# Holding back the PSUM eviction of the first MLP product, and splitting the first weight tiles in halves

## The chip, the core and the metric

The kernel runs on one core of a Trainium2 chip. The metric is the device time of one execution in microseconds (us), lower is better. Matrix products run on TensorE, which has a queue for weight loads beside the one for matmuls (PEld and PE in the profile). ScalarE (ACT) and VectorE (DVE) do the elementwise work, SyncE (SP) issues nearly all loads, and every engine works through its own instructions in a fixed order. TensorE writes into PSUM banks, from which ScalarE and VectorE take the results.

## What is computed

The reference is a decoder trunk of two layers for 256 tokens and a width of 2048. Only the MLP part and the frame around it matter here:

```
def _sqrelu_mlp(h, w1, w2):
    return jnp.square(jax.nn.relu(h @ w1)) @ w2

def reference(x, ...):
    for l in range(DEPTH):            # DEPTH = 2
        h = _rmsnorm(x, norm1_g[l])
        ...                           # layer 0: convolution and differential attention
        ...                           # layer 1: forgetting attention
        h = _rmsnorm(x, norm2_g[l])
        x = x + _sqrelu_mlp(h, mlp_w1[l], mlp_w2[l])   # hidden width 8192
    return x
```

## The kernel before

All products are made with float32 accuracy out of a fast format: each operand is split into a high part and a low part, and three matmuls (high by high, high by low, low by high) are added up in PSUM. For a weight tile `raw` of 1 MB, `split_w` writes the high part `wh` on ScalarE (line 136) and the low part `wl` on VectorE (line 137). There are three buffers each for `raw`, `wh` and `wl`, so a split waits until TensorE has finished with the tile three places earlier, and a load waits until the tile three places earlier is split.

The MLP (`mlp`) goes over the hidden width in four groups `g` of 2048. In each group `hidden` makes the first product in eight pairs of 128-column blocks: `gemm_t` loads and splits two weight tiles per pair, runs their matmuls (lines 548 and 552) and leaves two PSUM banks `acc[0]` and `acc[1]`. Taking them out is called eviction here. It is a copy on ScalarE (line 597) and an add on VectorE (line 598) for each bank, then ReLU and square in one VectorE instruction (line 600), then `p.fill`, which splits the result for the second product (for the last pair lines 582 and 583):

```
fj = f[:, 2 * j:2 * j + 2].rearrange("p t n -> p (t n)")
nc.scalar.copy(fj, acc[j][:, 2 * P:])
nc.vector.tensor_tensor(fj, acc[j][:, :2 * P], fj, ALU.add)
```

The second product (`gemm_pair`) follows, twice per group, for `n` = 0 and `n` = 2. It goes over the same eight pairs, one weight tile each. Pairs of kind S use a product scheme with seven products instead of eight. It needs sums of weight blocks, a tile `T` that VectorE builds in three instructions (lines 632, 634, 635) and that is split like a weight tile. So an S tile has two splits, `wa` of the loaded tile and `wb` of `T`. On TensorE an S tile is 21 matmuls (lines 615 to 617), of which the first nine use `wa` and the other twelve `wb`; a C tile is 24. The tiles come in the order S C S C S C C C, 183 matmuls in all. Four banks, `P2`, `Q3`, `Q4` and `X`, come from the same pool of four as the `acc` banks of the first product: `Q4` and `X` are the two that the last pair of `hidden` has just filled.

`late` is a list of work that is postponed; `flush()` does it. `gemm`, `gemm_t` and `gemm_pair` call `flush()` behind the split of their first weight tile and ahead of their first matmul. A scheduler then orders the instructions of each engine; it keeps to the data but may move an instruction past others. So the order of the program is not simply the order of the code.

At the start of the kernel the first product loads its first weight tile in two halves (`first=True`, line 150) but splits it in one piece.

Of the kernel before, what the change touches and what calls it, by code (L numbers as in the profile page):

```python
# [8 lines left out]
F32 = mybir.dt.float32  # L9
F32R = mybir.dt.float32r  # L10
AF = mybir.ActivationFunctionType
ALU = mybir.AluOpType
# [4 lines left out]
P = 128  # L17
D = 2048
KT = D // P
CW = 512  # L20
# [6 lines left out]
def trunk_kernel(  # L27
# [7 lines left out]
    nc = tc.nc  # L35
# [6 lines left out]
    qkv = ctx.enter_context(tc.tile_pool(name="qkv", bufs=2))  # L42
# [34 lines left out]
    late = []  # L77

    def flush():

        while late:
            late.pop(0)()

    def step():

        while pending:
            try:
                next(pending[0])
                return True
            except StopIteration:  # L90
                pending.pop(0)
        return False

    def until(done):
        while not done():
            assert step()
# [31 lines left out]
                nc.vector.scalar_tensor_tensor(lo, src, scalar, hi.bitcast(F32), ALU.mult, ALU.subtract)  # L128
            self.left -= n

    def split_w(src, shape=(4, CW)):

        n = src.shape[1]
        wh = wspl.tile([P, *shape], F32R, name="wh")[:, :n]
        wl = wspl.tile([P, *shape], F32R, name="wl")[:, :n]
        nc.scalar.copy(wh, src)  # L136
        nc.vector.tensor_tensor(wl, src, wh.bitcast(F32), ALU.subtract)  # L137
        return wh, wl

    def gemm(acts, w, c0, first=False):  # L140

        acc = []
        total = 4 * len(acts)
        i = 0
        for ai, a in enumerate(acts):
            raw = wraw.tile([P, 4, CW], F32, name="raw")
            src = w[a.row:a.row + CW, c0:c0 + CW].rearrange("(k p) n -> p k n", p=P)
            if first and ai == 0:
                for h in range(2):
                    nc.sync.dma_start(raw[:, 2 * h:2 * h + 2, :], src[:, 2 * h:2 * h + 2, :])  # L150
            else:
                nc.sync.dma_start(raw, src)
            wh, wl = split_w(raw)
            if i == 0:
                flush()
                acc += [accp.tile([P, CW], F32, name="acc") for _ in range(2)]
            until(lambda: a.left <= 0)
            for h in range(2):
                for t in range(2):
                    ts = slice(t * P, (t + 1) * P)  # L160
                    for k in (2 * h, 2 * h + 1):
                        st, sp = i + k == 0, i + k == total - 1
                        nc.tensor.matmul(acc[t], a.hi[:, k, ts], wh[:, k, :], start=st, stop=False)  # L163
                        nc.tensor.matmul(acc[t], a.hi[:, k, ts], wl[:, k, :], start=False, stop=False)  # L164
                        nc.tensor.matmul(acc[t], a.lo[:, k, ts], wh[:, k, :], start=False, stop=sp)  # L165
                step()
            i += 4
        return acc
# [38 lines left out]
    def proj(nm, w, c0, name, first=False):  # L207

        acc = gemm(nm.acts, w, c0, first)
        if name == "q":  # L210
            qk_tile.append(qkv.tile([P, 4, CW], F32, name="qk"))
        o = qkv.tile([P, 2, CW], F32, name="v") if name == "v" else \
            qk_tile[-1][:, (0 if name == "q" else 2):(2 if name == "q" else 4), :]
        for t in range(2):
            nc.scalar.activation(o[:, t, :], acc[t], AF.Copy, scale=nm.r(t))
        return o
# [302 lines left out]
    def out_proj(acts, w, nxt):  # L519

        for part in (acts[:-1], acts[-1:]):
            for n in range(NCH):
                acc = gemm(part, w, n * CW)
                for t in range(2):
                    nc.vector.tensor_tensor(xr[n][:, t, :], acc[t], xr[n][:, t, :], ALU.add)
                if len(part) == 1:
                    pending.append(nxt.chunk(n))

    def gemm_t(acts, w, c0):


        acc = []
        for c in range(2):
            raw = wraw.tile([P, 8, 2 * P], F32, name="raw")
            r0 = c * 8 * P
            nc.sync.dma_start(raw, w[r0:r0 + 8 * P, c0:c0 + 2 * P].rearrange("(k p) n -> p k n", p=P))
            wh, wl = split_w(raw, (8, 2 * P))
            if c == 0:
                flush()
                acc += [accp.tile([P, CW], F32, name="acc") for _ in range(2)]  # L540
            for h in range(2):
                a = acts[2 * c + h]
                until(lambda: a.left <= 0)
                for f in range(2):
                    fs = slice(f * P, (f + 1) * P)
                    for k in range(4):
                        st = c + h + k == 0
                        nc.tensor.matmul(  # L548
                            acc[f], wh[:, 4 * h + k, fs], a.both[:, k, :, :].rearrange("p s t -> p (s t)"), start=st, stop=False)
                    for k in range(4):  # L550
                        sp = (c, h, k) == (1, 1, 3)
                        nc.tensor.matmul(acc[f][:, 2 * P:], wl[:, 4 * h + k, fs], a.hi[:, k, :], start=False, stop=sp)  # L552
                step()
        return acc
# [34 lines left out]
    def hidden(nm, w, c0):  # L589

        pairs, half = [], None
        for i, kind in enumerate(KINDS):
            acc = gemm_t(nm.acts, w, c0 + 2 * i * P)
            f = qkv.tile([P, 4, CW], F32, name="qk")[:, :2].rearrange("p a (f n) -> p (a f) n", n=P)
            for j in range(2):
                fj = f[:, 2 * j:2 * j + 2].rearrange("p t n -> p (t n)")
                nc.scalar.copy(fj, acc[j][:, 2 * P:])  # L597
                nc.vector.tensor_tensor(fj, acc[j][:, :2 * P], fj, ALU.add)  # L598
            f4 = f[:, :4].rearrange("p t n -> p (t n)")
            nc.vector.scalar_tensor_tensor(f4, f4, 0.0, f4, ALU.max, ALU.mult)  # L600
            if kind == "S":
                p = PairS()
            elif half is not None:
                p, half = PairC(half), None
            elif "C" in KINDS[i + 1:]:
                t = actp.tile([P, 4, 2, 2 * P], F32R, name="act")
                p, half = PairC(t[:, :2]), t[:, 2:]
            else:
                p = PairC(qkv.tile([P, 2, 2, 2 * P], F32R, name="v"))
            p.fill(f)  # L610
            pairs.append(p)
        return pairs

    def products(acc, a, b, started, last):
# [4 lines left out]
    def gemm_pair(pairs, w, r0, n, r2, done):  # L619
# [3 lines left out]
        for i, (kind, p) in enumerate(zip(KINDS, pairs)):  # L623
# [6 lines left out]
            if kind == "S":  # L630
                T = qkv.tile([P, 4, CW], F32, name="qk")
                nc.vector.tensor_tensor(
                    T[:, 0:2], raw[:, 1:3], raw[:, 0:1].broadcast_to([P, 2, CW]), ALU.add)
                nc.vector.tensor_tensor(T[:, 2], T[:, 1], raw[:, 1], ALU.add)
                nc.vector.tensor_tensor(T[:, 3], T[:, 2], raw[:, 3], ALU.add)  # L635
                wa, wb = split_w(raw[:, 1:4]), split_w(T)
            else:
                wa = split_w(raw)
# [41 lines left out]
    def mlp(nm, l, nxt):  # L680
        ov = out[0].rearrange("(t p) d -> p t d", p=P)
        r2 = None
        for g in range(4):
            pairs = hidden(nm, mlp_w1[l], g * D)
            if g == 0:
                r2 = small.tile([P, 2], F32, name="r2", bufs=3)
                for t in range(2):
                    nc.vector.tensor_tensor(r2[:, t:t + 1], nm.r(t), nm.r(t), ALU.mult)
            for n in (0, 2):
                def done(stage, m=None, t=None, n=n, g=g):  # L690
                    if g != 3:
                        return
                    if nxt is None:
                        if stage == 1:
                            q = nc.sync if t == 0 else nc.scalar
                            q.dma_start(ov[:, t, m * CW:(m + 1) * CW], xr[m][:, t, :])
                    elif n == 2 and stage == 0:
                        pending.extend([nxt.chunk(0), nxt.chunk(1)])
                    elif n == 2 and (m, t) == (n + 1, 1):
                        pending.extend([nxt.chunk(2), nxt.chunk(3)])  # L700
                gemm_pair(pairs, mlp_w2[l], g * D, n, r2, done)
        if nxt is None:
            flush()
# [72 lines left out]
```

## Time and profile before

| | before |
|---|---|
| device time, median of 3 runs | 2217.84 us (2216.75 to 2218.78) |
| device time of the profiled execution | 2219.12 us |
| its span, from the first to the last instruction | 2217.4 us |
| TensorE matmul busy | 2183.2 us (98%) |
| VectorE busy | 1544.1 us (70%) |
| ScalarE busy | 1051.0 us (47%) |

The profiled execution took 1.3 us longer than the median, and 1.7 us of it lie outside the span. A busy share of 98% says that TensorE has work almost always; it doesn't say that this work runs at full speed, since matmuls overlap and their recorded ends are modelled. Starts are better: in a dense stretch one matmul of 512 columns starts every 0.23 us at full clock. PEclk is the clock that TensorE was granted, as a share of 2.4 GHz.

### The profile page before, as it was taken

The page shows a single profiled execution, that of the slowest core. Times are in us where ns is not written, and L with a number is a line of the kernel's source. Part 1 is how long each engine was busy: PE and PEld are TensorE (multiplying, and loading weights), DVE is VectorE, ACT ScalarE, POOL GpSimd, SP SyncE. Part 2 cuts the span into 40 slices and gives each one's busy share as a digit, 9 for nine tenths or more (in the row PEclk, how much of TensorE's full clock was granted, in tenths as well). Part 3 has the DMA queues.
Part 4 walks back from the last instruction along what each step waited for, and adds up shares of the span by engine and source line. Part 5 has one row for each costly group of instructions (what it writes and reads, how often), then busy time and mean ns, then how long its engine had stood idle before and what let it go on. Part 6 is the DMA issues. An engine that isn't in the chain of part 4 may idle for free.

```text
span 2217.4 us, 25974 instructions
## 1 busy us (share of the span) xinstructions
PE 2183.2 (98%) x10724; PEld 1824.2 (82%) x10724; DVE 1544.1 (70%) x1568; ACT 1051.0 (47%) x1095; POOL 18.4 (1%) x17
## 2 busy tenths in 40 slices
PE   8999999999999999999999999999999999999999
PEld 6887888888887887887888888888888888878877
DVE  5576655768768768767855565657687687687677
ACT  5455444545435444444554455445454454444443
POOL 0000000000000000000000000000000000000000
PEclk9999999999999999999999999999999999999999
DMA  7544556546655665664646555556556556656654
GB/s 253 176 166 161 181 188 192 177 154 207 210 163 199 214 186 177 211 190 161 214 159 203 185 175 177 183 162 186 157 204 211 161 198 211 188 171 210 189 166 157
DMA packets 245240, 412.07 MB, mean 186 GB/s; under 512 B 9367, under 2 KB 144770, under 8 KB 245122
## 3 DMA queue, kind: packets, MB, share of 16 engines
q1 hardware_dynamic: 237264, 405.84, 56.9%
q10 hardware_dynamic: 7858, 4.58, 0.7%
q8 instruction: 84, 1.38, 0.2%
q14 instruction: 34, 0.28, 0.0%
HBM read 408.28 MB, written 2.11 MB: 185 GB/s over the span
## 4 chain that ended last, share of the span: by engine, by line
PE 96%; DVE 1%; ACT 1%; DMA 1%; issue 0%; ACTq 0%; DVEq 0%
PE acc L548 21%; PE acc L552 11%; PE acc L163 11%; PE acc L165 10%; PE acc L164 10%; PE acc L616 8%; PE acc L617 8%; PE acc L615 8%; PE tp L616 2%; PE tp L617 2%; PE tp L615 2%; ACT wh L136 1%; DVE wl L137 1%; PE tp L184 1%; PE tp L305 0%; PE tp L317 0%
## 5 line engine op out<-in xcount | busy, mean ns | idle before, releaser
L137 DVE TENSOR_TENSOR wl<-raw,wh 128x2048 fp32r<-128x2048 f32 (+1 forms) x384 | 853.5, 2223 | 453.1 <-ACT wh L136 452.7
L136 ACT CAST wh<-raw 128x2048 fp32r<-128x2048 f32 (+1 forms) x384 | 711.0, 1856 | 488.7 <-PE acc L165 218.7
L548 PE MATMUL acc<-act,wh 128*128 128x512 f32 x2048 | 559.5, 395 | 0.0
L163 PE MATMUL acc<-wh,act 128*128 128x512 f32 x1024 | 413.0, 404 | 0.3 <-ACT act L127 0.2
L164 PE MATMUL acc<-wl,act 128*128 128x512 f32 x1024 | 400.8, 391 | 0.0
L165 PE MATMUL acc<-wh,act 128*128 128x512 f32 x1024 | 400.7, 392 | 0.0
L548 PEld LDWEIGHTS acc<-act,wh 128*128 128x128 f32 x2048 | 350.3, 189 | 47.9 <-DVE act L128 0.6
L552 PEld LDWEIGHTS acc<-act,wl 128*128 128x128 f32 x2048 | 314.2, 189 | 43.4
L552 PE MATMUL acc<-act,wl 128*128 128x256 f32 x2048 | 325.7, 281 | 0.0
L616 PE MATMUL acc<-wl,act 128*128 128x512 f32 x656 | 257.2, 392 | 0.0
L617 PE MATMUL acc<-wh,act 128*128 128x512 f32 x656 | 255.8, 390 | 0.0
L615 PE MATMUL acc<-wh,act 128*128 128x512 f32 x656 | 245.8, 392 | 1.1 <-ACT wh L136 1.1
L165 PEld LDWEIGHTS acc<-wh,act 128*128 128x128 f32 x1024 | 192.5, 188 | 42.2 <-DVE act L128 0.4
L163 PEld LDWEIGHTS acc<-wh,act 128*128 128x128 f32 x1024 | 192.8, 188 | 39.2 <-issue 2.0
L164 PEld LDWEIGHTS acc<-wl,act 128*128 128x128 f32 x1024 | 193.2, 189 | 37.5 <-issue 0.7
L136 ACT CAST wh<-qk 128x2048 fp32r<-128x2048 f32 x48 | 91.7, 1910 | 211.3 <-DVE qk L635 211.3
L137 DVE TENSOR_TENSOR wl<-qk,wh 128x2048 fp32r<-128x2048 f32 x48 | 109.9, 2290 | 60.2 <-ACT wh L136 60.2
L615 PEld LDWEIGHTS acc<-wh,act 128*128 128x128 f32 x656 | 123.5, 189 | 28.8 <-ACT wh L136 2.8
L616 PEld LDWEIGHTS acc<-wl,act 128*128 128x128 f32 x656 | 123.8, 189 | 28.3 <-DVE wl L137 2.3
L617 PEld LDWEIGHTS acc<-wh,act 128*128 128x128 f32 x656 | 123.8, 189 | 25.7
L597 ACT COPY qk<-acc 128x256 f32<-128x256 f32 x128 | 47.0, 367 | 178.6 <-PE acc L552 178.6
L598 DVE TENSOR_TENSOR qk<-acc,qk 128x256 f32<-128x256 f32 x128 | 53.8, 420 | 54.7 <-ACT qk L597 54.7
(173 smaller groups left out, 1604.1 us busy)
## 6 DMA issues: line engine op xcount, KB each, us to landing
raw<-in_mlp_w_dram SPq DMA_DIRECT2D x256, 1024.0 KB, 5.4
raw<-in_fox_w_in_dram SPq DMA_DIRECT2D x48, 1024.0 KB, 5.1
raw<-in_hyb_w_in_dram SPq DMA_DIRECT2D x47, 1024.0 KB, 5.1
raw<-in_hyb_w_out_dram SPq DMA_DIRECT2D x16, 1024.0 KB, 5.1
raw<-in_fox_w_out_dram SPq DMA_DIRECT2D x16, 1024.0 KB, 5.1
ob<-fcd ACTq DMA_DIRECT2D x4, 512.0 KB, 4.6
xr<-in_x_dram SPq DMA_DIRECT2D x3, 512.0 KB, 8.1
raw<-in_hyb_w_in_dram SPq DMA_DIRECT2D x2, 512.0 KB, 6.8
```

What stands on the lines that cost most here:

```text
L136: nc.scalar.copy(wh, src)
L137: nc.vector.tensor_tensor(wl, src, wh.bitcast(F32), ALU.subtract)
L163: nc.tensor.matmul(acc[t], a.hi[:, k, ts], wh[:, k, :], start=st, stop=False)
L164: nc.tensor.matmul(acc[t], a.hi[:, k, ts], wl[:, k, :], start=False, stop=False)
L165: nc.tensor.matmul(acc[t], a.lo[:, k, ts], wh[:, k, :], start=False, stop=sp)
L548: nc.tensor.matmul(acc[f], wh[:, 4 * h + k, fs], a.both[:, k, :, :].rearrange("p s t -> p (s t)"), start=st, stop=False)
L552: nc.tensor.matmul(acc[f][:, 2 * P:], wl[:, 4 * h + k, fs], a.hi[:, k, :], start=False, stop=sp)
L597: nc.scalar.copy(fj, acc[j][:, 2 * P:])
L598: nc.vector.tensor_tensor(fj, acc[j][:, :2 * P], fj, ALU.add)
L615: nc.tensor.matmul(acc, a[0], b[0], start=not started, stop=False)
L616: nc.tensor.matmul(acc, a[0], b[1], start=False, stop=False)
L617: nc.tensor.matmul(acc, a[1], b[0], start=False, stop=last)
```

## The change

In `hidden`, the eviction of a pair becomes a function `take`, which is put on `late`. It is thus done by the next `flush()`: for pairs 0 to 6 behind the split of the next pair's first weight tile, and for pair 7 in `gemm_pair`, behind the splits of `wa` and `wb` of the second product's first tile. In `split_w`, a tile can be split in parts, and the four tiles of the kernel's first product (`first=True`) are split in two halves each.

```
-    def split_w(src, shape=(4, CW)):
+    def split_w(src, shape=(4, CW), parts=1):
...
-        nc.scalar.copy(wh, src)
-        nc.vector.tensor_tensor(wl, src, wh.bitcast(F32), ALU.subtract)
+        for i in range(parts):
+            s = slice(i * n // parts, (i + 1) * n // parts)
+            nc.scalar.copy(wh[:, s], src[:, s])
+            nc.vector.tensor_tensor(wl[:, s], src[:, s], wh[:, s].bitcast(F32), ALU.subtract)
         return wh, wl
...
-            wh, wl = split_w(raw)
+            wh, wl = split_w(raw, parts=2 if first else 1)
...
             acc = gemm_t(nm.acts, w, c0 + 2 * i * P)
-            f = qkv.tile([P, 4, CW], F32, name="qk")[:, :2].rearrange("p a (f n) -> p (a f) n", n=P)
-            for j in range(2):
...
-            p.fill(f)
             pairs.append(p)
+
+            def take(acc=acc, p=p):
+                f = qkv.tile([P, 4, CW], F32, name="qk")[:, :2].rearrange("p a (f n) -> p (a f) n", n=P)
+                for j in range(2):
+                    fj = f[:, 2 * j:2 * j + 2].rearrange("p t n -> p (t n)")
+                    nc.scalar.copy(fj, acc[j][:, 2 * P:])
+                    nc.vector.tensor_tensor(fj, acc[j][:, :2 * P], fj, ALU.add)
+                f4 = f[:, :4].rearrange("p t n -> p (t n)")
+                nc.vector.scalar_tensor_tensor(f4, f4, 0.0, f4, ALU.max, ALU.mult)
+                p.fill(f)
+            late.append(take)
         return pairs
```

Lines behind the two edits move by 2 and by 5 in the changed kernel: 136 and 137 become 138 and 139; the eviction's 597, 598 and 600 become 611, 612 and 614; 583 becomes 585; 632, 634 and 635 become 637, 639 and 640.

The first place is VectorE's order at the border between the two products, in the first group of the first MLP; it is the same in all eight groups. `qk` is the name of the buffers both of the evicted result `f` and of `T`. Before, from the split of the second product's first loaded tile on (1536 columns):

```order
L137 TENSOR_TENSOR wl<-raw,wh 128x1536
L598 TENSOR_TENSOR qk<-acc,qk 128x256
L600 SCALAR_TENSOR_TENSOR qk<-qk 128x512
L583 TENSOR_TENSOR act<-qk,act 128x2x256
L632 TENSOR_TENSOR qk<-raw 128x1024
L598 TENSOR_TENSOR qk<-acc,qk 128x256
L634 TENSOR_TENSOR qk<-qk,raw 128x512
L598 TENSOR_TENSOR qk<-acc,qk 128x256
L635 TENSOR_TENSOR qk<-qk,raw 128x512
L600 SCALAR_TENSOR_TENSOR qk<-qk 128x512
L137 TENSOR_TENSOR wl<-qk,wh 128x2048
L583 TENSOR_TENSOR v<-qk,v 128x2x256
```

In the changed kernel, from the sums of `T` of the first tile on:

```order
L637 TENSOR_TENSOR qk<-raw 128x1024
L612 TENSOR_TENSOR qk<-acc,qk 128x256
L639 TENSOR_TENSOR qk<-qk,raw 128x512
L640 TENSOR_TENSOR qk<-qk,raw 128x512
L612 TENSOR_TENSOR qk<-acc,qk 128x256
L139 TENSOR_TENSOR wl<-raw,wh 128x1536
L614 SCALAR_TENSOR_TENSOR qk<-qk 128x512
L585 TENSOR_TENSOR act<-qk,act 128x2x256
L139 TENSOR_TENSOR wl<-qk,wh 128x2048
```

The two adds among these rows (612) are now those of pair 6, whose banks were full one pair earlier. The adds of pair 7 follow only behind the split of `T` (`wl<-qk`), in this order:

```order
L637 TENSOR_TENSOR qk<-raw 128x1024
L612 TENSOR_TENSOR qk<-acc,qk 128x256
L639 TENSOR_TENSOR qk<-qk,raw 128x512
L640 TENSOR_TENSOR qk<-qk,raw 128x512
L139 TENSOR_TENSOR wl<-raw,wh 128x2048
L612 TENSOR_TENSOR qk<-acc,qk 128x256
L139 TENSOR_TENSOR wl<-raw,wh 128x1536
L614 SCALAR_TENSOR_TENSOR qk<-qk 128x512
L139 TENSOR_TENSOR wl<-qk,wh 128x2048
L585 TENSOR_TENSOR v<-qk,v 128x2x256
```

So what moved is pair 7's eviction, from between the sums of the first `T` to behind its split; it now stands among the sums of the third tile's `T` and the splits of the second and third tile. For pairs 0 to 6 the scheduler already had this order.

The second place is VectorE at the kernel's start. `g_95` and `ob` are gains and small constants, line 128 (unchanged) splits activations. Before:

```order
L128 SCALAR_TENSOR_TENSOR act<-tp,g_95,act 128x256 x4
L137 TENSOR_TENSOR wl<-raw,wh 128x2048
L128 SCALAR_TENSOR_TENSOR act<-tp,g_95,act 128x256 x4
L137 TENSOR_TENSOR wl<-raw,wh 128x2048 x2
L128 SCALAR_TENSOR_TENSOR act<-tp,g_95,act 128x256 x2
```

In the changed kernel:

```order
L128 SCALAR_TENSOR_TENSOR act<-tp,g_95,act 128x256 x3
L139 TENSOR_TENSOR wl<-raw,wh 128x1024
L128 SCALAR_TENSOR_TENSOR act<-tp,g_95,act 128x256
L139 TENSOR_TENSOR wl<-raw,wh 128x1024
L128 SCALAR_TENSOR_TENSOR act<-tp,g_95,act 128x256 x2
L139 TENSOR_TENSOR wl<-raw,wh 128x1024 x2
```

Each split of the first product is now two instructions of half the width, with activation splits between them.

## Rows read from the trace of the kernel before

**Rows 1.** The page, busy time, share of the span and instructions of TensorE.
```profile
PE 2183.2 (98%) x10724; PEld 1824.2 (82%) x10724; DVE 1544.1 (70%) x1568; ACT 1051.0 (47%) x1095; POOL 18.4 (1%) x17
```

**Rows 2.** Waits of TensorE: waiting line, releaser, us in total, times, longest.
```profile
PE tp L615 <- ACT wh L136: 10.9, 8, 1.4
PE tp L616 <- DVE wl L137: 9.1, 8, 1.1
```

**Rows 3.** Windows over second products and one pair before: stretch, us, busy (instructions), PEclk, DMA share, GB/s.
```profile
487.30:532.62 45.32, 42.52 (x185) 1.00 0.59 199
...
2124.36:2171.80 47.44, 44.94 (x185) 0.93 0.56 190
sum 367.03, PE 345.91; mean PE 43.24
...
532.62:574.33 41.71, 41.71 (x184) 1.00 0.65 212
...
476.07:487.30 11.23, 11.23 (x67) 1.00 0.24 86
```

**Rows 4.** Timeline, TensorE: start, us, instruction, idle before and releaser.
```profile
487.30 0.40 PE L615 MATMUL tp<-wh,act 128*128 128x512 f32 x1
...
490.91 0.96 PE L615 MATMUL tp<-wh,act 128*128 128x512 f32 x3 [1.39 <-ACT wh L136]
...
493.24 0.50 PE L616 MATMUL tp<-wl,act 128*128 128x512 f32 x1 [1.14 <-DVE wl L137]
```

**Rows 5.** Timeline, VectorE, around the same border.
```profile
472.40 2.29 DVE L137 TENSOR_TENSOR wl<-raw,wh 128x2048 fp32r<-128x2048 f32 x1 [1.12 <-ACT wh L136]
...
477.31 1.76 DVE L137 TENSOR_TENSOR wl<-raw,wh 128x1536 fp32r<-128x1536 f32 x1 [1.56 <-ACT wh L136]
...
481.54 1.23 DVE L632 TENSOR_TENSOR qk<-raw 128x1024 f32<-128x1024 f32 x1
486.55 0.42 DVE L598 TENSOR_TENSOR qk<-acc,qk 128x256 f32<-128x256 f32 x1 [3.78 <-ACT qk L597]
486.89 0.68 DVE L634 TENSOR_TENSOR qk<-qk,raw 128x512 f32<-128x512 f32 x1
487.90 0.42 DVE L598 TENSOR_TENSOR qk<-acc,qk 128x256 f32<-128x256 f32 x1 [0.33 <-ACT qk L597]
488.25 0.68 DVE L635 TENSOR_TENSOR qk<-qk,raw 128x512 f32<-128x512 f32 x1
...
490.89 2.29 DVE L137 TENSOR_TENSOR wl<-qk,wh 128x2048 fp32r<-128x2048 f32 x1 [1.36 <-ACT wh L136]
```

**Rows 6.** Timeline, ScalarE, around the same border.
```profile
487.50 0.37 ACT L597 COPY qk<-acc 128x256 f32<-128x256 f32 x1 [0.98 <-PE acc L552]
488.96 1.90 ACT L136 CAST wh<-qk 128x2048 fp32r<-128x2048 f32 x1 [1.09 <-DVE qk L635]
```

**Rows 7.** Timeline, SyncE's queue: loads of the second product's third and fourth tile.
```profile
474.72 14.64 SPq L625 DMA_DIRECT2D raw<-in_mlp_w_dram  x2
```

**Rows 8.** The page: one group of ScalarE, two of loads (KB, median us to landing).
```profile
L570 ACT CAST act<-qk 128x1024 fp32r<-128x1024 f32 x24 | 25.1, 1045 | 0.0
...
raw<-in_mlp_w_dram SPq DMA_DIRECT2D x256, 1024.0 KB, 5.4
...
raw<-in_hyb_w_in_dram SPq DMA_DIRECT2D x2, 512.0 KB, 6.8
```

**Rows 9.** Timeline of the kernel's start, several engines.
```profile
2.18 0.94 SPq L150 DMA_DIRECT2D raw<-in_hyb_w_in_dram  x2
...
9.91 1.90 ACT L136 CAST wh<-raw 128x2048 fp32r<-128x2048 f32 x1 [1.66 <-DMA raw<-in_hyb_w_in_dram]
...
11.84 2.29 DVE L137 TENSOR_TENSOR wl<-raw,wh 128x2048 fp32r<-128x2048 f32 x1 [2.99 <-ACT wh L136]
...
14.22 0.78 PE L164 MATMUL acc<-wl,act 128*128 128x512 f32 x1
...
32.46 0.29 DVE L269 TENSOR_TENSOR y<-ob 128x128 f32<-128x128 f32 x1 [2.65 <-DMA ob<-in_hyb_lk_dram]
```

More of the change, by code (lines that the diff above doesn't have):

```diff
@@ L593, in hidden @@
             acc = gemm_t(nm.acts, w, c0 + 2 * i * P)
-            f = qkv.tile([P, 4, CW], F32, name="qk")[:, :2].rearrange("p a (f n) -> p (a f) n", n=P)
-            for j in range(2):
[L596 to L600, printed above, removed]
             if kind == "S":
```

## The prediction

> **What bounds the kernel now.** The page comes first: TensorE is busy for 2183.2 us of the span, 98% [rows 1]. Whatever doesn't shorten TensorE's own path is hidden, so I ask where TensorE stands still. The view of its waits has two large entries, and both belong to the second MLP product: eight waits for the high part of a split weight tile, 10.9 us in all, and eight for the low part, 9.1 us [rows 2]. There are eight groups (two layers of four), so this is one place that comes back eight times.
>
> To see what one place costs, idle time is not enough, because a matmul behind a gap starts slowly and the clock may fall. I therefore set windows from the first matmul of `gemm_pair` with n = 0 to the first with n = 2, and compare them with a window over n = 2, which has the same 183 matmuls and no wait: 41.71 us, or 0.228 us each. The eight windows over n = 0 add up to 367.03 us against 8 x 41.71 = 333.68 us [rows 3]. **33.35 us** are lost there. Four windows ran at granted clock 1.00 and look like the first (45.32 us), the other four were below, down to 0.93 in the last: part of their matmuls ran at 1.2 GHz instead of 2.4 GHz, after a gap. That part is 367.03 - 8 x 45.32 = 4.5 us.
>
> The chain behind a wait is in the timelines. I count from the first matmul of the second product (487.30) as zero [rows 4]. VectorE begins the sums of the first `T` at -5.8 (481.54), but its next instruction is the add of pair 7's first bank, which TensorE has not finished: VectorE sits idle for 3.78 us and adds at -0.75. The second add, at +0.60, stands ahead of the last sum, which starts at +0.95 [rows 5]. The add waits for ScalarE's copy at +0.20, and only at +1.66 can ScalarE split `T`, in 1.90 us [rows 6]; VectorE's low part is ready at +5.9 [rows 5]. TensorE needs `T` after nine matmuls, at 9 x 0.228 = 2.05, gets the high part at +3.61 and the low part at +5.94 [rows 4]. So the eviction, two adds of 0.42 us, delays `T` only because it is queued ahead of `T` and must wait for the end of the first product.
>
> **The change at the eight borders.** Nothing is added or removed; pair 7's adds go behind the split of `T`. I replay VectorE's new order with the old durations.
> - The last weight split of the first product ends at 472.40 + 2.29, that is -12.6 [rows 5]. Then come 1.23 + 0.42 + 0.68 + 0.68 us of sums and an add of pair 6, whose bank is long full: `T` is complete at about -9.6.
> - `wa` takes 1.76 us [rows 5]; with pair 6's second add and its rest, about 2.2 us at 0.4 to 0.7 us each, VectorE is at -5.4. ScalarE can write `T`'s high part once TensorE frees the buffer of the tile before the last of the first product. A first-product tile is half a pair, and the last pair ran 11.23 us [rows 3], so this is at -5.6. 1.90 us later, at about -3.9, VectorE starts the low part and ends at -1.6. TensorE needs it at +2.05. **The wait is gone with 3.6 us to spare.**
> - What is late next? Now the sums of the third tile's `T` and the first add of pair 7 follow, 3.0 us, until +1.4. The second tile's split can't start before TensorE frees its buffer at 0: the high part is there at +1.9, the low part at 1.9 + 2.29 = +4.2. TensorE asks for it after 21 matmuls and one more, at +5.0: 0.8 us to spare. Bank `Q4` is free at about 0 and due at 18 x 0.228 = 4.1; bank `X` is free behind the second add at +4.6 and due at 27 x 0.228 = 6.2.
> - Next VectorE needs 1.76 + 0.7 + 2.29 + 0.7 us for the third tile and the rest of pair 7, until about +10.0, in time for 10.3 (`wa`) and 12.3 (`T`). Then come the fifth tile's sums, ahead of the fourth tile's split. Their load starts when the second tile is split, at +4.2, and lands 5.4 us later [rows 8], at +9.6, so nothing waits. Sums until +12.6, split until +14.9, needed at 67 x 0.228 = 15.3: 0.4 us to spare.
>
> So all 33.35 us should come back, the clock's share included, but two margins are below 1 us, and the profile has no row of such an order. The bounds are 0 and 1.0 us per border, the size of a margin missed, 0 to 8 us. I take 1.5 us, near the low end, because every step of the replay met its time.
>
> **The change at the start.** The halves of the first weight tile are issued at 2.18 and about 0.5 us later [rows 9] and land after 6.8 us in the middle [rows 8]; the second has landed at 9.91, when ScalarE starts [rows 9], 7.2 us after its issue. The first then took 6.4 us and landed at 8.6. A half is 1.05 us on ScalarE [rows 8] and 1.23 us on VectorE, like the sum of 1024 columns [rows 5], so the first low part is ready at 10.9. Before, dense matmuls began at 14.22 [rows 9]. The upper bound is 3.3 us. The lower bound is -1: the other three tiles pay twice for starting an instruction, and the order around them changes. For a later step stands in the way: VectorE's line 269 waited 2.65 us for small loads, ahead of the fifth tile's split [rows 9]. The changed order issues these loads no earlier, behind more ScalarE work, so a TensorE that comes earlier waits for that split. I take 1.0 us, 3.3 less roughly that wait.
>
> The Trainium skill, page "Perfetto Trace Analysis", section "Optimizing Scalar/DVE Operations", advises breaking up ScalarE or VectorE instructions that make gaps on another engine, since work is then done sooner. Taken alone it would give the whole 3.3 us, and a sum of 2184.0 us; the row of line 269 is why I don't follow it here.
>
> **The sum.** Against the profiled execution's own 2219.1 us: -33.35 + 1.5 - 1.0 = -32.85, so **2186 us**. The median before is 1.3 us below that execution; some of this may be the clock's share, which comes and goes between executions and disappears with the gaps. Against the median it is -1.4%. What a measurement can tell from no change is about 0.2%, 4.4 us.
>
> **The rivals.**
> - *Part of the wait comes back at the next tiles.* VectorE is busy for some 40 of the 45 us of a border window, and the margins above are 0.8 and 0.4 us. If the second and fourth tile's splits slip by 1 to 2 us, TensorE waits 1 to 1.5 us in each of eight places, and the clock's 4.5 us may stay: 2186 - 1.5 + 8 to 12 + up to 4.5, that is 2193 to 2201 us. For it: sums now stand ahead of both splits. Against it: each step is on time in the replay. The same page, section "Optimizing Tensor Performance", wants the eviction of a bank to overlap the next group's matmuls in other banks; holding it back could make `Q4` and `X` late. By that mechanism the banks have 4.1 and 1.6 us to spare.
> - *Nothing is gained*, because the full wait moves to the second tile: 2215 to 2220 us. The replay would have to be off by 4 us.
> - *Slower.* VectorE's sums of the third tile wait for a load and now stand ahead of the second tile's split and of pair 7's adds; in a queue worked in order all of it waits. That load is issued at 474.72, -12.6 [rows 7]; with 5.4 us [rows 8] it lands at -7.2, and the sums are due at -1.6. To cost more than today's 4.2 us per border, the second tile's split must end 4.2 us behind +5.0 and so start at +6.9; the sums, 3.0 us, would start at +3.9. That is a landing 16.5 us after the issue, three times the median. At 18 us each border would lose about 5.7 us, 1.5 more than now: 2219.1 + 8 x 1.5 - 1.0 = 2230 us.
>
> **Chances.** The forecast, 2181 to 2190, gets 0.80; part of the wait coming back 0.13; nothing gained 0.04; slower 0.03. So faster 0.93, same 0.04, slower 0.03. The range reaches down to 2219.1 - 33.35 - 3.3 - 1.3 = 2181 (no rest of the waits, the whole gain at the start, and the profiled run's excess), and up to 2219.1 - 33.35 + 8 + 4.5 = 2198 (both margins missed, half clock as now, nothing from the start).
>
> **What would show it.** Right: TensorE's two entries of 10.9 and 9.1 us are gone; windows over n = 0 are 41.7 to 42 us long at clock 1.00; VectorE's last sum of the first `T` starts about 10 us ahead of the first matmul; the dense matmuls begin near 11. Wrong: new waits of TensorE for the second or fourth tile's low part, for a bank in `Q4` or `X`, or VectorE waiting for a load in the third tile's sums; at the start, a wait for the fifth tile's split longer than the gain.

## Result and the profile after

| | before | after |
|---|---|---|
| device time, median | 2217.30 us (2214.25 to 2218.78, 4 runs) | 2183.74 us (2182.76 to 2183.87, 4 runs) |
| profiled execution, its span | 2219.12, 2217.4 us | 2182.76, 2181.0 us |

The ratio is 0.9849, 95% interval 0.9832 to 0.9867. The change makes the kernel 1.5% faster; 2186 us (2181 to 2198) was forecast.

The page of the changed kernel, TensorE's busy time first, as in [rows 1]:

```profile
PE 2168.9 (99%) x10724; PEld 1822.0 (84%) x10724; DVE 1546.9 (71%) x1572; ACT 1053.6 (48%) x1099; POOL 18.8 (1%) x17
```

All its waits of TensorE that the view lists, as in [rows 2] (who waits, releaser, us in total, times, longest):

```profile
PE tp L65 <- DMA ident<-eye_dram: 2.8, 1, 2.8
PE acc L166 <- DVE wl L139: 2.3, 1, 2.3
PE acc L165 <- ACT wh L138: 1.7, 1, 1.7
PE tp L186 <- DMA xr<-in_x_dram: 1.6, 1, 1.6
```

The two entries of 10.9 and 9.1 us are gone. What is left in the view belongs to the first 40 us. Busy time fell by only 14.3 us while the span fell by 36.4: matmuls at half clock and behind a gap also count as busy, so the busy share hid the loss.

Windows over the eight second products with n = 0, TensorE alone, as in [rows 3], and the first with n = 2:

```profile
486.55:528.08 41.53, 41.53 (x185) 1.00 0.57 194
...
2094.12:2135.66 41.54, 41.54 (x186) 1.00 0.58 194
sum 332.92, PE 332.92; mean PE 41.61
```

```profile
528.08:569.56 41.48, 41.48 (x184) 1.00 0.63 211
```

Every window ran at granted clock 1.00, none is longer than 41.77, and their sum fell from 367.03 to 332.92 us: **34.11 us** come from here.

VectorE at the first border, in the order of the changed kernel (the first matmul of the second product is at 486.55):

```profile
476.05 0.69 DVE L640 TENSOR_TENSOR qk<-qk,raw 128x512 f32<-128x512 f32 x1
...
477.18 1.75 DVE L139 TENSOR_TENSOR wl<-raw,wh 128x1536 fp32r<-128x1536 f32 x1
...
482.66 2.29 DVE L139 TENSOR_TENSOR wl<-qk,wh 128x2048 fp32r<-128x2048 f32 x1 [1.75 <-ACT wh L138]
484.99 1.22 DVE L637 TENSOR_TENSOR qk<-raw 128x1024 f32<-128x1024 f32 x1
...
488.23 2.29 DVE L139 TENSOR_TENSOR wl<-raw,wh 128x2048 fp32r<-128x2048 f32 x1 [0.36 <-ACT wh L138]
490.44 0.42 DVE L612 TENSOR_TENSOR qk<-acc,qk 128x256 f32<-128x256 f32 x1
...
496.37 1.22 DVE L637 TENSOR_TENSOR qk<-raw 128x1024 f32<-128x1024 f32 x1
...
498.99 2.29 DVE L139 TENSOR_TENSOR wl<-raw,wh 128x2048 fp32r<-128x2048 f32 x1
```

`T` is complete 9.8 us ahead of the first matmul (before, the last sum began 0.95 us behind it, [rows 5]), and its low part ends at 484.95, 1.6 us ahead. Pair 7's second add stands at 490.44, behind the second tile's split.

The kernel's start, TensorE and VectorE:

```profile
9.59 0.79 PE L166 MATMUL acc<-wl,act 128*128 128x512 f32 x1
10.18 0.63 PE L167 MATMUL acc<-wh,act 128*128 128x512 f32 x1
10.61 0.63 PE L165 MATMUL acc<-wh,act 128*128 128x512 f32 x1
...
39.14 0.50 PE L166 MATMUL acc<-wl,act 128*128 128x512 f32 x1 [2.29 <-DVE wl L139]
```

```profile
36.27 0.29 DVE L271 TENSOR_TENSOR y<-ob 128x128 f32<-128x128 f32 x1 [4.15 <-DMA ob<-in_hyb_lk_dram]
...
36.80 2.28 DVE L139 TENSOR_TENSOR wl<-raw,wh 128x2048 fp32r<-128x2048 f32 x1
```

Dense matmuls begin 4.63 us earlier than in [rows 9], but line 271 (269 before) waits 4.15 us for the small loads, the fifth tile's split stands behind it, and TensorE stands still until 39.14. At the first border 0.75 us of the lead are left (486.55 against 487.30). The loads also come later than before. The issue of the last of them on ScalarE's queue, before and after:

```profile
27.79 0.77 ACTq L243 DMA_DIRECT2D ob<-in_hyb_lk_dram  x1
```

```profile
29.17 0.44 ACTq L245 DMA_DIRECT2D ob<-in_hyb_lk_dram  x1
```

It was issued 1.4 us later and took longer to land, so this product of `ob` ran at 36.27 where it had run at 32.46 ([rows 9]), and the fifth tile's split began at 36.80 where it had begun at 33.65.

So 36.4 us of span are 0.75 at the start, 34.11 in the windows over n = 0, and 1.5 in the windows over n = 2: some 0.2 us in seven of the eight, in the first 41.71 before and 41.48 now.

These two executions lie far apart: the profiled one before was slower than all four of the table, and the profiled one after is the fastest of its four. Between the medians the time fell by 33.6 us.

### The profile page after: what moved, and what is told of

The parts are those of the page before. It is cut to its first block, busy times and chain, and to the rows that moved or that the text cites. A ratio compares the mean times of both kernels' runs of the same rounds, so it can differ in the third digit from the quotient of the medians.

```text
span 2181.0 us, 26007 instructions
## 1 busy us (share of the span) xinstructions
PE 2168.9 (99%) x10724; PEld 1822.0 (84%) x10724; DVE 1546.9 (71%) x1572; ACT 1053.6 (48%) x1099; POOL 18.8 (1%) x17
## 4 chain that ended last, share of the span: by engine, by line
PE 99%; DMA 0%; DVE 0%; ACT 0%; issue 0%; SPq 0%; ACTq 0%; DVEq 0%
PE acc L550 22%; PE acc L554 11%; PE acc L165 11%; PE acc L167 11%; PE acc L166 11%; PE acc L621 8%; PE acc L622 8%; PE acc L620 8%; PE tp L622 2%; PE tp L620 2%; PE tp L621 2%; PE tp L186 1%; PE tp L307 0%; PE tp L319 0%; PE tp L495 0%; DMA ob<-in_hyb_lk_dram 0%
## 5 line engine op out<-in xcount | busy, mean ns | idle before, releaser
L139 DVE TENSOR_TENSOR wl<-raw,wh 128x2048 fp32r<-128x2048 f32 (+2 forms) x388 | 853.6, 2202 | 485.9 <-ACT wh L138 485.3
L138 ACT CAST wh<-raw 128x2048 fp32r<-128x2048 f32 (+2 forms) x388 | 712.8, 1839 | 595.4 <-PE acc L167 219.2
L621 PE MATMUL tp<-wl,act 128*128 128x512 f32 x192 | 74.8, 389 | 0.0
```

The costliest lines, as they stand in the source:

```text
L138: nc.scalar.copy(wh[:, s], src[:, s])
L139: nc.vector.tensor_tensor(wl[:, s], src[:, s], wh[:, s].bitcast(F32), ALU.subtract)
L621: nc.tensor.matmul(acc, a[0], b[1], start=False, stop=False)
```

## The experiments

First a point on order alone, read from the built programs and not from runs. If pairs 0 to 6 are evicted at once and only pair 7 is put on `late`, TensorE, VectorE, ScalarE and SyncE have row for row the order of the changed kernel; so they have if pair 7 is then flushed, at n = 0, just behind the sums of `T`, or between the two splits. So what matters is that pair 7's eviction is written behind the sums of `T`; at which of these three places does not.

**1 and 2: each half of the change alone.** The first keeps `take` and splits tiles whole, the second has `parts` on the kernel before:

```
-            wh, wl = split_w(raw, parts=2 if first else 1)
+            wh, wl = split_w(raw, parts=1)
```

> Only the eviction is held back; the first weight tiles are split in one piece, as before. My theory: the eight borders give all of 34.1 us of window time and the start gives 0.75 us, read at the first border (486.55 against 487.30), and the two are independent. Then this kernel takes 2183.7 + 0.75 = 2184.5 us, TensorE has none of its sixteen border waits, and the first border is at 487.3. Rival: the halves bring more than the first border shows (up to the 4.6 us by which the first dense matmul came earlier), then it takes 2186 to 2188 us. Second rival: the halves bring nothing or cost something, then 2183.0 to 2183.7 us.

> Only the first four weight tiles are split in halves; the eviction stands as before. My theory: all sixteen border waits of TensorE are there again, 20 us of idle time, and the eight windows over n = 0 sum to about 367 us; the start gives 0.75 us, so 2217.3 - 0.75 = 2216.5 us, no difference that a comparison can tell. At the start the first dense matmul is at about 9.6 and TensorE stands still for some 2.3 us near 39 behind the small loads. Rival: the whole 4.6 us of the earlier first matmul stay, then 2212.7 us.

The eviction alone: 2184.51 us (2183.48 to 2184.88), ratio 0.9847 [0.9834, 0.9861]. The halves alone: 2220.66 us (2217.89 to 2222.83, 11 runs), ratio 1.0013 [1.0004, 1.0022]. All of the gain is the eviction's. With it alone, none of the sixteen border waits is left; all that the view still lists behind the start is:

```profile
PE acc L621 <- DVE wl L139: 1.8, 3, 0.8
```

But the first border tells more: it is at 485.92 without halves, earlier than with them. With the halves alone it is at 487.92. The 0.75 us at the start are thus no gain of the halves, as I had expected for these two runs; they lie within the spread of the start.

The halves alone cost 3.7 us by the medians, where I had expected a gain of 0.8; the start has 0.6 of it. Waits of TensorE there, and windows over n = 0, TensorE alone:

```profile
PE tp L617 <- ACT wh L138: 10.9, 8, 1.4
PE tp L618 <- DVE wl L139: 10.2, 9, 1.1
```

```profile
487.92:534.04 46.12, 43.60 (x186) 0.96 0.59 195
...
1595.13:1640.39 45.26, 42.48 (x186) 1.00 0.60 199
1771.91:1819.35 47.44, 44.94 (x185) 0.93 0.57 189
1950.85:1997.60 46.75, 42.88 (x185) 1.00 0.58 192
...
sum 369.86, PE 348.20; mean PE 43.53
```

The windows sum to 369.86 - 367.03 = 2.8 us more than before; with the 0.6 at the start these are the 3.4 us by which the spans differ. Two things make them up. There is one wait more, of 1.1 us for a low part in the window from 1950.85, which is 1.5 us longer than 45.26 at the same clock of 1.00. And six of eight windows are below clock 1.00, where before it was four; that leaves some 1.3 us for the clock. So the clock's share of the border waits varies. The eleven executions had mean granted clocks of 0.994 to 0.997, the fifteen of the kernel before beside them 0.995 to 0.998. So the share was larger with the halves in most; why is open.

The eviction alone also shows the thin place of the new order. Two of the three waits for a low part lie in its windows over n = 0 (0.79 and 0.39 us; a third, of 0.60, in one over n = 2); the longest, at the second border, TensorE and VectorE:

```profile
675.05 0.50 PE L621 MATMUL acc<-wl,act 128*128 128x512 f32 x1 [0.79 <-DVE wl L139]
```

```profile
670.11 1.23 DVE L637 TENSOR_TENSOR qk<-raw 128x1024 f32<-128x1024 f32 x1 [1.35 <-DMA raw<-in_mlp_w_dram]
...
672.71 3.95 DVE L139 TENSOR_TENSOR wl<-raw,wh 128x2048 fp32r<-128x2048 f32 x2
```

The fifth tile's load landed 7.2 us after its issue (at 662.86); its sums waited for it and stand ahead of the fourth tile's split, so TensorE waited at the fourth tile. In the changed kernel the same load took 6.3 us at this border, VectorE waited 0.44 us, and TensorE lost 0.2.

**3 and 4: the small loads earlier.** The four loads of `ob` go to GpSimd's queue, or to the head of ScalarE's:

```
         for i, v in enumerate((hyb_lq1, hyb_lk1, hyb_lq2, hyb_lk2)):
-            nc.scalar.dma_start(lv[:, i, :], v.broadcast_to([P, 64]))
+            nc.gpsimd.dma_start(lv[:, i, :], v.broadcast_to([P, 64]))
```

> The changed kernel, with the four small loads of ob put on GpSimd's queue, where they are the first work, instead of on ScalarE's queue behind the first tiles' splits. VectorE's product of ob (line 271) then stands ahead of all weight splits. My theory: the start gave back 2.8 us of its lead at 39.14 because line 271 waited 4.15 us for these loads, ahead of the fifth tile's split. With the loads landed early the lead of about 3.3 us at the 96th matmul stays, the wait of 2.29 us for wl is gone, and the kernel takes 2183.7 - 2.5 = 2181.2 us (2180.5 to 2182). Rival: TensorE, weight loads or another split is late at the same place anyway, and the kernel takes 2183.5 us as it does now. Second rival: the small loads land after the first half tile, or delay it, so that line 271 holds up the first splits: 2184 to 2188 us.

> The changed kernel, with the four small loads of ob issued first on ScalarE's own queue, ahead of the other small loads. The fourth is issued behind the second half's split, near 9.6, and line 271 stands behind the low part of the second half, near 11. My theory: a queue worked in order passes on the wait of its head; the fourth load lands 5 to 8 us after its issue, at 15 to 18, while VectorE's next instruction was due at 15.2, so between 0 and 3 us of the start are lost there, and the 2.3 us at 39 are won back: 2181 to 2184 us, with the first border between 483.5 and 486.6. Rival: the start is limited by the loads of the weight tiles alone, and the time is 2183.5 us wherever line 271 stands.

On GpSimd's queue: 2185.26 us (2183.69 to 2185.89), the second rival. VectorE and TensorE there:

```profile
10.62 0.29 DVE L271 TENSOR_TENSOR y<-ob 128x128 f32<-128x128 f32 x1 [9.65 <-DMA ob<-in_hyb_lk_dram]
```

```profile
13.60 0.80 PE L166 MATMUL acc<-wl,act 128*128 128x512 f32 x1 [2.04 <-DVE wl L139]
```

The last of the loads was issued at 3.04 and had landed by 10.62; line 271 stood ahead of everything on VectorE, so the first split came late. At the head of ScalarE's queue: **2181.43 us** (2180.66 to 2182.29), 2.3 us below the changed kernel, as my theory had it.

**5: `T` tied to the end of the first product, the eviction still held back.**

```
+                if i == 0 and n == 0:
+                    nc.vector.scalar_tensor_tensor(
+                        T[:, 3, 0:1], last[1][:, 0:1], 0.0, T[:, 3, 0:1], ALU.mult, ALU.add)
```

> The changed kernel with one tiny VectorE instruction added for the first tile of n = 0: one column of T's last block takes in 0 times one column of the last pair's second bank. The eviction stays held back in the code; only T's split is tied to the end of the first product, and the first add goes ahead of the tie. My theory: what cost 33 us was that T was finished behind the end of the first product, not the adds' own 0.84 us. T is then complete at about +0.4 from the first matmul of the second product, ScalarE's high part at +0.6 to +2.5, VectorE's low part at +4.8, while TensorE needs it at +2.3: 2.5 us lost per border, 20 us in all, and up to 4 us of half clock: 2183.7 + 20 to 24 = 2204 to 2208 us. Rival: the eviction's work among the sums was the cost, or VectorE's total work there; then a one-column instruction changes nothing: 2184 us.

2214.05 us (2212.93 to 2215.79), ratio 0.9982 [0.9972, 0.9991]: nearly all the gain is gone. The rival is out, but my figure was 6 to 10 us too low. VectorE at the first border (first matmul at 487.22), and the windows over n = 0:

```profile
487.42 0.16 DVE L644 SCALAR_TENSOR_TENSOR qk<-acc,qk 128x1 f32<-128x1 f32 x1 [0.57 <-PE acc L555]
489.55 2.29 DVE L140 TENSOR_TENSOR wl<-qk,wh 128x2048 fp32r<-128x2048 f32 x1 [1.97 <-ACT wh L139]
...
492.10 2.28 DVE L140 TENSOR_TENSOR wl<-raw,wh 128x2048 fp32r<-128x2048 f32 x1
494.30 0.68 DVE L616 SCALAR_TENSOR_TENSOR qk<-qk 128x512 f32<-128x512 f32 x1
494.90 1.22 DVE L639 TENSOR_TENSOR qk<-raw 128x1024 f32<-128x1024 f32 x1
```

```profile
487.22:532.27 45.05, 43.05 (x185) 1.00 0.53 177
...
sum 361.69, PE 344.37; mean PE 43.05
```

TensorE at the first border:

```profile
491.64 0.74 PE L622 MATMUL acc<-wh,act 128*128 128x512 f32 x2 [0.87 <-ACT wh L139]
492.22 0.39 PE L623 MATMUL tp<-wl,act 128*128 128x512 f32 x1
```

The low part of `T` ends at +4.6, as expected (+4.8); the first matmul with it starts at 492.22. The wait of 0.87 us just before is for the high part of the second tile, which ScalarE makes behind that of `T`. Counted at 0.2267 us per matmul (41.48 us for 183), TensorE has lost 1.6 us of the first border at 492.22, and it loses another 1.9 us at the third tile: the scheduler put its sums (494.90) behind the second tile's split, so a second `T` is late. This run thus shows that a late `T` costs time without an add ahead of its sums, 1.6 of 3.5 us per border; the rest is a change of order that the tie brought along.

**6 and 7: a delay in front of the second tile's low part,** two and four VectorE instructions (`pad`) between `wh` and `wl`:

```
+            for k in range(pad):
+                nc.vector.tensor_tensor(work.tile([P, CW], F32, name="junk"), wh[:, k].bitcast(F32), src[:, k], ALU.subtract)
```

> The changed kernel with two VectorE instructions of 512 columns (0.68 us each, results unused) between the second tile's high part and its low part, in each n = 0: 1.36 us of delay where the replay had 0.8 us to spare and the changed kernel's trace 1.02 us. My theory: TensorE waits 0.3 us for the second tile's low part; the fifth tile's load, issued when the second tile is split, is 1.4 us later, its sums stand ahead of the fourth tile's split, and TensorE waits about 1 us more there: 1.3 us per border, 10 us in all, 2192 to 2198 us with some half clock. Rival (the margins are really wide, the delay is caught by VectorE's idle time of 0.36 and 0.43 us and by TensorE's own queue): 2184 to 2186 us.

> As the kernel with two added instructions, with four: 2.7 us of delay ahead of the second tile's low part. My theory: TensorE waits 1.7 us for the second tile's low part and about 1 us more for the fourth's: 2.7 us per border, 21 us, and half clock in some borders: 2204 to 2212 us, most of the change's gain. Rival (wide margins, as above): 1 us per border at most, below 2192 us.

Two: 2188.96 us (2188.62 to 2189.77), between both expectations. Four: 2206.94 us (2204.94 to 2207.83), as my theory had it. The windows over n = 0 sum to 337.43 and 355.28 us, 0.6 and 2.8 us more per border than in the changed kernel. VectorE and TensorE with four, first border (first matmul at 487.44):

```profile
493.06 3.95 DVE L141 TENSOR_TENSOR wl<-raw,wh 128x2048 fp32r<-128x2048 f32 x2
496.94 2.28 DVE L141 TENSOR_TENSOR wl<-qk,wh 128x2048 fp32r<-128x2048 f32 x1
501.62 1.23 DVE L639 TENSOR_TENSOR qk<-raw 128x1024 f32<-128x1024 f32 x1 [2.41 <-DMA raw<-in_mlp_w_dram]
```

```profile
494.44 0.98 PE L622 MATMUL tp<-wh,act 128*128 128x512 f32 x3 [0.92 <-ACT wh L138]
505.83 0.50 PE L623 MATMUL acc<-wl,act 128*128 128x512 f32 x1 [1.07 <-DVE wl L141]
```

The second tile is split later, the fifth tile's load is issued later and lands later (2.41 us of waiting), its first two sums hold up the fourth tile's split, and TensorE waits at both tiles. The wait at 494.44 is for the high part of the third tile's `T`: in this order some of the third tile's matmuls stand ahead of those with the second tile's low part. That low part ends at 495.3, and with its first matmul (495.40) TensorE has lost 1.4 us. 2.7 us of delay cost 2.8. With two, TensorE passed the second tile at a loss of 0.3 us, and the scheduler put the fourth tile's split ahead of the last sum of the fifth; that saved most of the microsecond I had put there.

**8 to 11: the start once more, on one chip.** The changed kernel again, the small loads first with whole tiles (`parts=1`), with halves for the first tile alone, and with halves for four tiles:

```
-            wh, wl = split_w(raw, parts=2 if first else 1)
+            wh, wl = split_w(raw, parts=2 if first and ai == 0 else 1)
```

> The changed kernel once more, unchanged, beside the three that follow, to see how far its start varies between executions. My theory: the borders are the same in every execution (windows over n = 0 of 41.5 to 41.8 us) and only the landing of the first loads differs, by 1 to 1.5 us: 2183 to 2185 us, with a stall of TensorE of 2 to 2.3 us for the fifth tile's low part near 39.

> The four small loads issued first on ScalarE's queue, the first weight tiles split in one piece. All four loads are here issued ahead of the first split; line 271 stands ahead of the first tile's low part. My theory: without halves the stall at 39 was not there anyway (only the wait of 1.04 us of VectorE in the kernel with the eviction alone), so the early loads bring little and cost a wait if they land behind 9.9: 2184 to 2187 us. Rival: halves don't matter at all and the early loads alone bring the 2.3 us: 2181 to 2182 us.

> The small loads first, and only the first weight tile split in halves, not the next three. My theory: the gain of the halves comes from the first tile, whose halves land apart; in the next three each extra pair of instructions costs 0.2 us on an engine that is not the bound there, so 2181 to 2182 us as with four tiles in halves. Rival: the halves of the second to fourth tile shorten a wait of TensorE too, then 2182.5 to 2184 us.

> The kernel with the small loads first and four tiles in halves once more, beside the changed kernel on one chip. My theory: it stays 1.5 to 2.5 us below the changed kernel, 2181 to 2182 us, since TensorE's stall near 39 is gone. Rival: the difference was the spread of the start between executions, then both are within 0.5 us of each other.

| | median us (range, runs) | first border | sum over n = 0 |
|---|---|---|---|
| 8, changed kernel | 2184.68 (2182.79 to 2184.97, 5) | 488.27 | 332.88 |
| 9, loads first, whole tiles | 2185.38 (2184.21 to 2187.30, 4) | 489.23 | 332.62 |
| 10, loads first, first tile halved | 2183.28 (2182.15 to 2183.80, 4) | 485.89 | 333.24 |
| 11, loads first, four tiles halved | 2181.77 (2180.82 to 2182.09, 4) | 484.59 | 333.24 |

The borders are the same in all four; the start alone makes the difference. The first borders follow the times, and the ranges of 8 and 11 don't touch: **the small loads first, with the halves, beat the changed kernel by 2.3 to 2.9 us**, ratio 0.9834 [0.9818, 0.9849] to the kernel before. Without early loads the halves gave nothing (1 against 8). Run 9 came within its range (2184 to 2187), but it does not tell what the early loads give without halves, since its order also put line 271 ahead of the first low part, where it waited 4.04 us until 12.87. In 10 my theory fell: it is 1.5 us slower than 11, so the halves of tiles two to four do count. In 10 TensorE waits 0.75 us for a low part at 20.65, in 11 it has no such wait. That row of 10, and then VectorE in 11:

```profile
20.65 0.50 PE L166 MATMUL acc<-wl,act 128*128 128x512 f32 x1 [0.75 <-DVE wl L139]
```

```profile
15.81 0.29 DVE L271 TENSOR_TENSOR y<-ob 128x128 f32<-128x128 f32 x1 [3.38 <-DMA y<-in_norm_g_dram]
```

VectorE still waits 3.38 us here (the view names the load issued just behind the four), but early, with little queued behind it; the fifth tile's split stands no longer behind it, and the view of waits has no entry for the low part near 39.

## Why the prediction was right, and where its terms were off

Between the profiled executions the time fell by 2219.12 - 2182.76 = 36.36 us; the sum said 32.85. Between the medians it fell by 33.56, so most of this difference lies in which executions were profiled. The terms below are measured on the profiled pair.

- **The place and the cause.** Right. All sixteen waits at the borders are gone, and the eviction alone gives the whole gain (1): that moving pair 7's eviction behind the sums removes the loss is shown. That a `T` held back by the end of the first product costs time is shown by itself for a part of the loss (5). For the kernel before, the chain from the adds through `T` to TensorE is read from its rows ([rows 4] to [rows 6]).
- **The replay.** It met nearly every step. In us from the first matmul of the second product, at the first border:

| step | replay | measured |
|---|---|---|
| `T` complete | -9.6 | -9.8 |
| `T`'s low part begins, ends | -3.9, -1.6 | -3.9, -1.6 |
| second tile's low part ends | +4.2 | +4.0 |
| fifth tile's sums begin | +9.6 | +9.8 |
| fourth tile's low part ends | +14.9 | +14.7 |

At six of the eight borders the fifth tile's sums began only at +10.2 to +10.4, after 0.3 to 0.5 us of waiting for their load. The replay's "so nothing waits" thus failed there by about the 0.4 us it had to spare.

- **-33.35 us at the eight borders.** 34.11 measured, and 1.5 more in the windows over n = 2. The term took the window over n = 2 as free of loss; at 41.48 us now, it had 0.2 us in it. The clock's share went with the gaps: eight windows at 1.00.
- **+1.5 us for waits that remain.** Mis-sized: in the changed kernel's profile the view has none. In the eight profiles with this order at the borders (the changed kernel, runs 1, 3, 4 and 8 to 11) the windows over n = 0 sum to 332.6 to 334.8 us, so a rest of 0 to 2 us; only run 1 comes near 1.5. The two thin margins were real, though. The one of 0.4 us at the fourth tile failed in places in run 1 (waits of 0.79 and 0.39 us); both failed under the delays of runs 6 and 7. The banks `Q4` and `X`, at which the rival's rule on eviction pointed, never show as a wait.
- **-1.0 us at the start.** The number came out (-0.75), by luck; the reason did not. The earlier first matmul was right: in the six profiles with this start (the changed kernel, runs 2 and 5 to 8) dense matmuls begin 3.2 to 4.6 us ahead of [rows 9], against 3.3 forecast. What failed is the step "I take 1.0 us, 3.3 less roughly that wait". It named the wait of line 269 rightly, but sized it as it was before, 2.65 us. With the halves the loads are issued and land later (line 271 at 36.27, not 32.46), and TensorE stands still for 2.2 to 2.8 us near 40 in all six. Nothing is left for the halves: the six first borders are 486.55 to 488.27, those without halves 487.30 ([rows 4]) and 485.92 (run 1). The halves are worth 0 within about 1 us as long as the loads stay where they are.
- The sum of 2184.0 us, by the rule of the Trainium skill on breaking up instructions (page "Perfetto Trace Analysis", section "Optimizing Scalar/DVE Operations"), lies nearer to 2183.74 than mine. Yet run 1 without halves took 2184.51: the number agreed, not its reason. What the halves need is line 271 out of the way, as in run 11.
- **The misses add up:** 1.5 (no rest of waits) + 0.8 (windows over n = 0) + 1.5 (windows over n = 2) - 0.25 (start) = 3.5, the 36.36 - 32.85 us.
- **The rivals.** "Part of the wait comes back" is what runs 6 and 7 bring about, at the two tiles it named; in the changed kernel it didn't happen. For "slower" the third tile's load had to land 16.5 us after its issue; VectorE waited for it at none of the eight borders.

## What to carry to other kernels

An instruction that must wait for the end of a stage, queued ahead of work for the next stage that could be done already, costs the whole chain behind it; write it behind, then replay the engine's new order with old durations and look for the next thin margin. A busy share of 98% doesn't exclude such a loss: compare the length of a window with that of a like one without waits. An engine that comes earlier to a place only gains if whatever else is queued in front of its next input comes earlier too: move the small loads together with the splits, and measure both parts alone.

## What the runs showed of the hardware

- **The clock's share of a gap varies.** Idle gaps of 1.39 and 1.14 us at a border ([rows 4]) came with granted clock 1.00 in four of eight windows and 0.93 to 0.96 in four before, 1.00 in two of eight with the halves alone. In runs 5 to 7, whose waits at the borders are 1.2 us or less, all windows read 1.00, though in run 5 seven borders lost 3.3 to 3.5 us each and one 4.6. Of the 14 executions of the kernel before beside those runs, five with a mean granted clock of 0.995 took 2219.5 to 2223.9 us, four with 0.998 took 2214.5 to 2217.6. With the gaps gone the changed kernel's two sets of executions spread over 1.1 and 2.2 us.
- **The first dense matmuls are slow.** In the changed kernel they start every 0.42 to 0.43 us from 10.18 to 14.02, the pace of 1.2 GHz, and every 0.23 us afterwards, though the window of the start reads a granted clock of 1.00. The Trainium skill (page "TensorE: Matmul & The Clock Gate", section "Wait — 56ns, not 53.3ns?") gives 426.7 ns from start to start for 512 columns at the lower clock, which agrees. Before, the pace changed near 16.8. An earlier start thus gave back 4.62 - 2.49 = 2.1 us of its lead between the sixth and the 48th matmul of the first product, in these and in transposes that moved in between.
- **The time of a small load varies.** Line 271 (269 before) waits for the four loads of `ob`, 64 floats per partition each. It started 7.1 us after the last of them was issued in the changed kernel (29.17 to 36.27) and 7.6 us in run 3 (3.04 to 10.62), no sooner than loads of 0.5 MB land (6.8 us, [rows 8]). In the kernel before it was 4.7 us (27.79 to 32.46), in run 1 3.1 us (27.23 to 30.29).
